# Summing one modulation vector off TensorE, and four others for one stream only

## The chip, the cores and the metric

The kernel runs on one core of a Trainium2 chip. The metric is the device time of one execution in microseconds (us). The kernel before took 1370.71 us, the median of three runs (1370.51 to 1374.48).

## What is computed

The reference is a block of two layers over two token streams of 256 tokens each: a latent stream `x` and a context stream `ctx`, 1024 channels wide. Layer 0 mixes tokens with a recurrence, layer 1 with a gated delta rule. Each is followed by a SwiGLU feed-forward part. Every sub-layer is modulated by vectors computed from `c` (latent) and `c_ctx` (context):

```python
for layer in range(DEPTH):                       # DEPTH = 2
    last = layer == DEPTH - 1
    mod_l = split((silu(c) @ ada_w[layer] + ada_b[layer])[:, None, :], 6)
    mod_c = split(silu(c_ctx) @ ada_w[layer] + ada_b[layer], 6)
    h_lat = modulate(rmsnorm(x, norm_g[layer, 0]), mod_l[0], mod_l[1])
    h_ctx = modulate(rmsnorm(ctx, norm_g[layer, 0]), mod_c[0], mod_c[1])
    ...                                          # the mixer gives y_lat, y_ctx
    x = x + mod_l[2] * y_lat
    x = x + mod_l[5] * swiglu(modulate(rmsnorm(x, norm_g[layer, 1]), mod_l[3], mod_l[4]), ...)
    if not last:
        ctx = ctx + mod_c[2] * y_ctx
        ctx = ctx + mod_c[5] * swiglu(...)
return rmsnorm(x, final_norm_g)
```

So each layer has six modulation vectors of 1024 channels for each of the two streams. Each is a product of an activation vector with a 1024 x 1024 slice of `ada_w`. In the last layer (layer 1) the context stream is read by the mixer but not carried on: vectors 0 and 1 of that layer are used for both streams, vectors 2 to 5 for the latent stream alone.

## The kernel before

Large products are made of three TensorE matmuls each (`mm3`): weights and activations are split into a high and a low part (`whi`/`wlo`, `hh`/`hl`), and high x high, high x low and low x high are summed. A weight tile of 128 x 1024 (512 KB) is loaded through SP's queue into one of three `raw` buffers, `whi` is a copy made on ScalarE or VectorE, `wlo` a subtraction made on VectorE or GpSimd (`weight`, line 704; two buffers of each). `product` (line 941) takes one such weight and runs 24 matmuls on it; with 512 tokens each is 128 x 512.

The program is recorded and then put in order in Python by a list scheduler (`Recorder`). It collects operations until a pool is closed (`flush`, line 391), chooses among the ready operations by an estimated time and their place in the program, and for operations with two possible engines (`scaled`: ScalarE or VectorE; `tt`: VectorE or GpSimd) also the engine. The order it gives on each engine, SP's DMA queue among them, is then fixed. All instructions are issued from one line, 612, so the profile's groups are told apart by the tiles they write and read.

Stages around the change: the first mixer (up to the close of pool `m0`, line 1095), whose end is the output projection, a norm and the first two weights of the feed-forward part; then the feed-forward part of layer 0, `ffn(0, ...)` (line 1098). It loops over 22 column tiles with a gate and an up product each (the first pair is made ahead, by `product2`), and then over eight output tiles of the down projection, each with weights of 8, 8 and 6 blocks, the last tile twice (once per half of the tokens). Its output is scaled by `mods[0][:, 5]` in `upd0`. Pool `fp` closes at line 1164; the second mixer follows.

The modulation vectors that are not needed at the very start are computed in the background. `ada_later(l, m...)` queues a generator `ada_steps(l, m)` per vector; each call of `product`, and each weight of a down projection, moves the first generator in the queue on by one step (`bg_step`). A vector has eight steps, one per 128 rows of its weight slice. A step loads 128 x 1024 of `ada_w` (512 KB) into a slot of `ring` (four slots in the first mixer, two in the feed-forward part) and then works in one of two ways:

- direct: four matmuls with the two activation columns (padded to 32) as the stationary operand, side by side in four column groups of TensorE, summed over the eight steps in one PSUM bank (`ps_ada<-ring,cs` in the profile);
- not direct: `acc` has one 128 x 1024 half for each stream (in the profile it goes by the name `x`, as it is part of the tile `x2`). The first step writes both halves by a scaling of the slot. Each later step does, for the latent stream, a multiply-add on VectorE; for the context stream, a scaling of the slot in place on ScalarE and an addition on VectorE or GpSimd. After the eighth step, eight matmuls with a selector as the stationary operand sum `acc` over the partitions (`ps_ada<-x,sel`).

The profile records each such 32-column matmul as two. Behind either way come a copy (`ada_ev`), two transposes (`ps_adat`) and an addition of the bias into `mods[l][:, m]`.

Before the change, vectors 2, 3, 4 and 5 of layer 0 are direct. (0,2) to (0,4) are queued with the mixer (line 1052). (0,5) is queued at line 1090; `bg_step(TUNE["g0"])`, with g0 = 4, records its first four steps in the first mixer's part, and the other four come in the feed-forward part. Layer 1's vectors 0 to 5 are queued at line 1131, not direct, and follow there.

Of the kernel before, what the change touches and what calls it, by code (L numbers as in the profile page):

```python
# [14 lines left out]
AF = mybir.ActivationFunctionType  # L15
OP = mybir.AluOpType
# [26 lines left out]
def _shuffle(sh, pattern, sizes):  # L43
# [18 lines left out]
    for g, n in zip(lhs, sh.shape, strict=True):  # L62
# [3 lines left out]
        for a in g:  # L66
# [7 lines left out]
TUNE = dict(warm=5000, ev=3000, stay=(300, 0), g0=4, early=(1, 2, 4, 6), eb=0, ea=(0, 1, 1, 1), nwo=2, prog=PROG,  # L74
            bias={'C3': -1500, 'N0': 100, 'N': -700, 'Z3': -1200, 'L': -1500, 'E3': 700, 'W': 10000, 'L3': -800, 'E': -300, 'W0': 10000, 'P': -100, 'E0': -300, 'N3': -700, 'P2': 0, 'C': 400, 'A': 700, 'Z': 700, 'C1': 0})
# [545 lines left out]
def hybrid_block(ctx: ExitStack, tc: tile.TileContext, I, out, dbg=None):  # L621
    nc = tc.nc
    ctx.enter_context(tc.manual_schedule())
    R = Recorder(tc, nc)
    T, V, S, G, sync = R.T, R.V, R.S, R.G, R.sync
# [14 lines left out]
    def bank(tag, name="ps"):  # L640
        if tag == "mm" and cur["wide"]:
            tag = ("mm", "tr", "st", "mm", "st", "tr", "st")[cur["turn"] % 7]
            cur["turn"] += 1
        return ps_pool.tile([128, 512], F32, tag=tag, bufs=banks[tag], name=name)

    def tmp(cols=512, dt=F32, name="tmp", tag="t2k", bufs=NB["t2k"]):
        t = tp.tile([128, 512], dt, tag=tag, bufs=bufs, name=name)
        return t[:, :cols] if cols != 512 else t
# [8 lines left out]
    def P(name):  # L657
        o, w = _SM[name]
        return sm[:, o:o + w]
# [23 lines left out]
    cs = cp.tile([128, NK, 32], F32, name="cs")  # L683
# [20 lines left out]
    def weight(*src, cols=1024, aside=False, place=None):  # L704

        r = raws.pop(0) if raws else raw_load(src, cols)
        hi, lo = place or (wp.tile([128, 1024], F32R, tag=t, bufs=NB[t], name=t) for t in ("whi", "wlo"))
        if aside:
            S.activation(hi[:, :cols], r[:, :cols], AF.Copy)
        else:  # L710
            R.copy(hi[:, :cols], r[:, :cols])
        (R.tt if (cur["wide"] or cur.get("flex")) and not aside else G.tensor_tensor)(lo[:, :cols], r[:, :cols], hi[:, :cols].bitcast(F32),
                                                                 OP.subtract)
        return hi, lo
# [3 lines left out]
    def ahead(*srcs):  # L718

        early.extend(weight(src, aside=True) for src in srcs)  # L720
# [13 lines left out]
    def ada_steps(l, m, direct=False):  # L734


        if l not in mods:
            mods[l] = cp.tile([128, 6, NK, 2], F32, name=f"mod{l}")
        if direct:
            ps = bank("ta", "ps_ada")  # L740
        for k in range(NK):
            r = next(cur["araw"])
            sync.dma_start(out=r, in_=I["ada_w"][l, m, k], after=cur["late"])
            if direct:
                for g in range(4):
                    T.matmul(ps[32 * g:32 * g + 32, 0:256], cs[:, k, :], r[:, 256 * g:256 * g + 256],
                             start=(k == 0), stop=(k == NK - 1))
            else:
                if k == 0:
                    acc = cur["acc"]  # L750
                    for v in range(2):
                        R.scaled(acc[:, v], r, cs[:, k, v:v + 1])
                else:
                    V.scalar_tensor_tensor(acc[:, 0], r, cs[:, k, 0:1], acc[:, 0], OP.mult, OP.add)
                    S.activation(r, r, AF.Copy, scale=cs[:, k, 1:2])
                    R.tt(acc[:, 1], acc[:, 1], r, OP.add)
            if k < NK - 1:
                yield
        if not direct:
            ps = bank("ta", "ps_ada")  # L760
            for v in range(2):
                for g in range(4):
                    T.matmul(ps[32 * g:32 * g + 32, 0:256], sel[:, v, :], acc[:, v, 256 * g:256 * g + 256],
                             start=(v == 0), stop=(v == 1))
        ev = tmp(256, name="ada_ev")
        S.activation(ev, ps[:, 0:256], AF.Copy)
        pt = bank("ta", "ps_adat")
        for t in range(2):
            T.transpose(pt[:, 128 * t:128 * t + 128], ev[:, 128 * t:128 * t + 128], ident)
        b = P("ada_b")[:, (l * 6 + m) * 8:(l * 6 + m) * 8 + 8]  # L770
        V.tensor_tensor(mods[l][:, m].rearrange("p (g t) v -> p g t v", t=2),
                        pt[:, 0:256].rearrange("p (t g c) -> p g t c", t=2, g=4)[:, :, :, 0:2],
                        b.rearrange("p (g t o) -> p g t o", t=2, o=1).to_broadcast([128, 4, 2, 2]), OP.add)
        yield

    def ada_later(l, *ms, direct=False):
        cur["bg"] += [ada_steps(l, m, direct) for m in ms]

    def bg_step(n=1):

        cur["quota"] -= n
        while n and cur["bg"] and cur["quota"] >= 0:
            if next(cur["bg"][0], "end") == "end":
                cur["bg"].pop(0)
            else:
                n -= 1
# [6 lines left out]
    def gain(l, which, m):  # L793
        a = cp.tile([128, NK, 2], F32, name=f"gain{l}{which}")
        o = (l * 2 + which) * 8
        V.scalar_tensor_tensor(a, mods[l][:, m], 1.0,
                               P("norm_g")[:, o:o + 8].rearrange("p (k o) -> p k o", o=1).to_broadcast([128, NK, 2]),
                               OP.add, OP.mult)
        return a
# [49 lines left out]
    def normed(xs, n, r, gn, shift, hh, hl):  # L849

        for i, c0 in enumerate(range(0, n, 256)):
            c = slice(c0, c0 + 256)
            for k in range(NK):
                ap, v = xs(k)[i]
                xg = tmp(256, name="xg")
                V.scalar_tensor_tensor(xg, ap, gn[:, k, v:v + 1], r[i], OP.mult, OP.mult)
                lift(k, c, xg, shift[:, k, v:v + 1], hh, hl)

    def both(t):
        return lambda k: [(t[:, k, 0:256], 1), (t[:, k, 256:512], 0)]  # L860
# [23 lines left out]
    for t in range(NK):  # L884
        ps = bank(("ta", "st")[t % 2], "ps_ada")
        for half in range(2):
            r = half_of[2 * t + half]
            sync.dma_start(out=r, in_=I["ada_w0"][t, half])
            for g in range(4):
                T.matmul(ps[32 * g:32 * g + 32, 0:256], cs[:, 4 * half + g, :], r[:, 256 * g:256 * g + 256],  # L890
                         start=half == 0, stop=half == 1)
# [195 lines left out]
        if len(parts) == 1:  # L1087
            r1.append(norm.part(cols.start))
    ahead(I["ffn_gu"][0, 0, 0], I["ffn_gu"][0, 1, 0])
    ada_later(0, 5, direct=True)  # L1090
    normed(both(x), 512, r1, gain(0, 1, 4), mods[0][:, 3], hh, hl)
    first = product2((I["ffn_gu"][0, 0, 0], I["ffn_gu"][0, 1, 0]), hh, hl)
    early.append(weight(I["ffn_gu"][0, 0, 1]))
    bg_step(TUNE["g0"])
    m0.close()


# [673 lines left out]
    r = norm.part(0)  # L1771
# [61 lines left out]
```

## Time and profile before

| | |
|---|---|
| three runs, median (lowest to highest) | 1370.71 us (1370.51 to 1374.48) |
| the profiled execution | 1377.74 us |
| its span, from the first to the last instruction | 1376.0 us |
| mean granted TensorE clock | 0.973 |
| busy share of the span: TensorE, VectorE, ScalarE, GpSimd | 96%, 77%, 43%, 18% |
| loads of `ada_w` | 96, of 512 KB |

How to read it: times are microseconds, engines are PE (TensorE matmuls), PEld (TensorE weight loads), DVE (VectorE), ACT (ScalarE), POOL (GpSimd) and SP (the queue that issues the DMAs). A row of the timeline has the start in us, the length in us, the engine, line, operation, written and read tiles, shape and count; in brackets stands the idle time of the engine before it and what ended that. A row of the table of stretches has the stretch, its length, the busy time and number of instructions of PE, PEld, DVE, ACT and POOL, the granted clock, the DMA share and GB/s. A row of one tile's instructions has the count, the shortest, median and longest duration in ns, and the first and last start in us. Matmuls overlap: the listed length of one is longer than the distance to the next.

### The profile page before, as it was taken

The page shows a single profiled execution, that of the slowest core. Times are in us where ns is not written, and L with a number is a line of the kernel's source. Part 1 is how long each engine was busy: PE and PEld are TensorE (multiplying, and loading weights), DVE is VectorE, ACT ScalarE, POOL GpSimd, SP SyncE. Part 2 cuts the span into 40 slices and gives each one's busy share as a digit, 9 for nine tenths or more (in the row PEclk, how much of TensorE's full clock was granted, in tenths as well). Part 3 has the DMA queues.
Part 4 walks back from the last instruction along what each step waited for, and adds up shares of the span by engine and source line. Part 5 has one row for each costly group of instructions (what it writes and reads, how often), then busy time and mean ns, then how long its engine had stood idle before and what let it go on. Part 6 is the DMA issues. An engine that isn't in the chain of part 4 may idle for free.

```text
span 1376.0 us, 23471 instructions
## 1 busy us (share of the span) xinstructions
PE 1324.9 (96%) x9280; PEld 1120.7 (81%) x9280; DVE 1055.5 (77%) x1856; ACT 591.5 (43%) x1078; POOL 247.3 (18%) x210
## 2 busy tenths in 40 slices
PE   6999999999999999999998999999998998999997
PEld 3677778778888888888867788898898888999997
DVE  5799986778887777457868889798599277777775
ACT  3388773334333333005745656747546341211100
POOL 2000000100121111212524333335243110000000
PEclk9999999999999999999999999999999599899999
DMA  9545443355555555233523222323133016355563
GB/s 356 193 166 179 139 152 121 122 179 191 203 179 184 186 192 172 84 111 124 173 75 124 74 78 79 107 82 107 61 119 117 20 55 206 131 184 184 180 181 115
DMA packets 61262, 195.62 MB, mean 142 GB/s; under 512 B 6752, under 2 KB 9952, under 8 KB 60896
## 3 DMA queue, kind: packets, MB, share of 16 engines
q1 hardware_dynamic: 61152, 194.12, 42.5%
q8 instruction: 73, 1.20, 0.4%
q14 instruction: 37, 0.30, 0.1%
HBM read 184.13 MB, written 9.96 MB: 141 GB/s over the span
## 4 chain that ended last, share of the span: by engine, by line
PE 56%; issue 16%; DVE 6%; ACT 3%; DMA 1%; POOL 0%; POOLq 0%; SPq 0%; ACTq 0%; DVEq 0%
PE ps_mm L612 28%; PE ps_dn L612 9%; PE ps_e L612 2%; PE ps_y L612 2%; PE ps_wo L612 2%; PE ps_z L612 2%; PE ps_w L612 2%; PE ps_s L612 2%; PE ps_ks L612 1%; DVE lw L612 1%; PE ps_a L612 1%; PE ps_qs L612 1%; DVE cu L612 1%; PE ps_o L612 1%; DMA ring<-ada_w 1%
## 5 line engine op out<-in xcount | busy, mean ns | idle before, releaser
L612 PE MATMUL ps_mm<-hh,whi 128*128 128x512 f32 (+1 forms) x888 | 328.3, 372 | 7.1 <-DVE cu L612 5.6
L612 PE MATMUL ps_mm<-hh,wlo 128*128 128x512 f32 (+1 forms) x888 | 327.8, 370 | 4.0 <-DVE wlo L612 2.3
L612 PE MATMUL ps_mm<-hl,whi 128*128 128x512 f32 (+1 forms) x888 | 327.1, 370 | 0.5 <-DVE hl L612 0.3
L612 DVE TENSOR_TENSOR wlo<-raw,whi 128x1024 fp32r<-128x1024 f32 (+2 forms) x185 | 233.8, 1264 | 21.6 <-ACT whi L612 13.3
L612 DVE CAST whi<-raw 128x1024 fp32r<-128x1024 f32 (+1 forms) x172 | 116.9, 679 | 129.2 <-PE ps_mm L612 68.7
L612 PEld LDWEIGHTS ps_mm<-hh,whi 128*128 128x128 f32 x888 | 170.3, 193 | 41.2 <-issue 9.6
L612 PEld LDWEIGHTS ps_mm<-hh,wlo 128*128 128x128 f32 x888 | 170.9, 193 | 33.8 <-DVE wlo L612 3.6
L612 PEld LDWEIGHTS ps_mm<-hl,whi 128*128 128x128 f32 x888 | 170.7, 193 | 26.5 <-issue 1.6
L612 POOL TENSOR_TENSOR wlo<-raw,whi 128x1024 fp32r<-128x1024 f32 x53 | 127.1, 2399 | 356.3 <-DVE whi L612 193.4
L612 PE MATMUL ps_dn<-fh,whi 128*128 128x256 f32 (+1 forms) x374 | 122.6, 328 | 0.0
L612 PE MATMUL ps_dn<-fl,whi 128*128 128x256 f32 (+1 forms) x374 | 122.6, 328 | 0.0
L612 PE MATMUL ps_dn<-fh,wlo 128*128 128x256 f32 (+1 forms) x374 | 122.3, 327 | 0.0
L612 PE MATMUL ps_mm<-h2h,whi 128*128 128x256 f32 x352 | 101.1, 288 | 1.1 <-ACT h2h L612 1.1
L612 PE MATMUL ps_mm<-h2l,whi 128*128 128x256 f32 x352 | 101.2, 287 | 0.0
L612 PE MATMUL ps_mm<-h2h,wlo 128*128 128x256 f32 x352 | 100.6, 286 | 0.0
L612 ACT ACTIVATE whi<-raw 128x1024 fp32r<-128x1024 f32 (+2 forms) x66 | 68.1, 1031 | 63.7 <-PE ps_mm L612 33.2
L612 ACT ACTIVATE fh<-sg 128x256 fp32r<-128x256 f32 (+1 forms) x43 | 22.5, 523 | 145.2 <-DVE sg L612 145.1
L612 ACT ACT_TABLE_LOAD x59 | 75.7, 1283 | 7.0 <-DMA sm<-small 3.4
L612 PEld LDWEIGHTS ps_dn<-fh,whi 128*128 128x128 f32 x374 | 71.1, 190 | 6.8 <-issue 0.4
L612 PEld LDWEIGHTS ps_dn<-fh,wlo 128*128 128x128 f32 x374 | 71.1, 190 | 6.1
L612 PEld LDWEIGHTS ps_dn<-fl,whi 128*128 128x128 f32 x374 | 71.1, 190 | 6.0
L612 ACT ACTIVATE ring<-ring,cs 128x1024 f32<-128x1024 f32 x42 | 48.3, 1150 | 64.4 <-DVE x L612 64.4
(326 smaller groups left out, 2637.9 us busy)
## 6 DMA issues: line engine op xcount, KB each, us to landing
ring<-ada_w SPq DMA_DIRECT2D x96, 512.0 KB, 4.5
raw<-ffn_gu SPq DMA_DIRECT2D x88, 512.0 KB, 3.6
raw<-dn_w_in SPq DMA_DIRECT2D x49, 512.0 KB, 3.5
raw<-ffn_down SPq DMA_DIRECT2D x34, 512.0 KB, 3.5
raw<-rg_w_in SPq DMA_DIRECT2D x16, 512.0 KB, 4.5
raw<-ffn_down SPq DMA_DIRECT2D x17, 384.0 KB, 3.4
raw<-dn_w_out SPq DMA_DIRECT2D x12, 512.0 KB, 3.9
raw<-rg_w_out SPq DMA_DIRECT2D x10, 512.0 KB, 3.5
```

The source lines that it names most:

```text
L612: call(*[real(x) for x in args], **{n: real(v) for n, v in kw.items()})
```

## The change

Vector (0,5) is no longer direct, and all its eight steps come in the feed-forward part, ahead of those of layer 1. For vectors 2 to 5 of layer 1, only the latent half of `acc` is computed and summed; the context columns of these vectors then hold the bias alone and are not read.

```diff
@@ ada_steps
+        nv = 1 if l == 1 and m >= 2 else 2
...
                 if k == 0:
                     acc = cur["acc"]
-                    for v in range(2):
+                    for v in range(nv):
                         R.scaled(acc[:, v], r, cs[:, k, v:v + 1])
                 else:
                     V.scalar_tensor_tensor(acc[:, 0], r, cs[:, k, 0:1], acc[:, 0], OP.mult, OP.add)
-                    S.activation(r, r, AF.Copy, scale=cs[:, k, 1:2])
-                    R.tt(acc[:, 1], acc[:, 1], r, OP.add)
+                    if nv == 2:
+                        S.activation(r, r, AF.Copy, scale=cs[:, k, 1:2])
+                        R.tt(acc[:, 1], acc[:, 1], r, OP.add)
...
-            for v in range(2):
+            for v in range(nv):
                 for g in range(4):
                     T.matmul(ps[32 * g:32 * g + 32, 0:256], sel[:, v, :], acc[:, v, 256 * g:256 * g + 256],
-                             start=(v == 0), stop=(v == 1))
+                             start=(v == 0), stop=(v == nv - 1))
@@ ahead of the feed-forward part
-    ada_later(0, 5, direct=True)
+    ada_later(0, 5)
     normed(both(x), 512, r1, gain(0, 1, 4), mods[0][:, 3], hh, hl)
     first = product2((I["ffn_gu"][0, 0, 0], I["ffn_gu"][0, 1, 0]), hh, hl)
     early.append(weight(I["ffn_gu"][0, 0, 1]))
-    bg_step(TUNE["g0"])
     m0.close()
```

## The prediction

> **What bounds the kernel now.** I read the page's busy line and slices first, then the busy time by stretch for the stages that the edit touches.
>
> ```profile
> PE 1324.9 (96%) x9280; PEld 1120.7 (81%) x9280; DVE 1055.5 (77%) x1856; ACT 591.5 (43%) x1078; POOL 247.3 (18%) x210
> ...
> 225.00:245.00 20.00, 20.00 (x149) 18.37 (x148) 15.65 (x23) 8.41 (x15) 3.87 (x3) 1.00 0.37 119
> 245.00:262.00 17.00, 14.55 (x97) 14.11 (x97) 15.26 (x38) 8.46 (x19) 3.07 (x3) 0.80 0.28 109
> 262.00:307.00 45.00, 42.98 (x208) 32.47 (x206) 28.84 (x33) 12.01 (x15) 2.41 (x1) 1.00 0.50 167
> 307.00:503.00 196.00, 196.00 (x911) 159.38 (x912) 158.14 (x152) 74.57 (x87) 30.50 (x12) 1.00 0.57 190
> 503.00:552.00 49.00, 49.00 (x241) 39.16 (x240) 36.93 (x41) 15.98 (x21) 6.60 (x3) 1.00 0.56 174
> ```
>
> TensorE (second column: busy PE) is full from 307 to 552 us, to the hundredth; from 262 to 307 it lacks 2.0 us. VectorE is at 81% there (158.14 of 196), ScalarE at 38%, the DMA at 57%. So in this stage, the first feed-forward part (about 262 to 630), only what leaves TensorE's own stream shortens the run. What matters for one matmul is its start-to-start distance, not its listed length:
>
> ```profile
> 325.61 0.39 PE L612 MATMUL ps_mm<-hh,whi 128*128 128x512 f32 x1
> 325.84 0.39 PE L612 MATMUL ps_mm<-hl,whi 128*128 128x512 f32 x1
> 326.07 0.39 PE L612 MATMUL ps_mm<-hh,wlo 128*128 128x512 f32 x1
> 326.29 0.39 PE L612 MATMUL ps_mm<-hh,whi 128*128 128x512 f32 x1
> ```
>
> Three steps take 0.68, one 0.227 us, though each is listed at 0.39. A product of 24 takes 5.44 us. Anything put between two of these costs the distance it adds.
>
> **The change part by part.**
>
> *The direct steps of vector (0,5) go.* There are eight, each with four calls, recorded as eight half-passes. Two of the three places:
>
> ```profile
> 194.23 0.39 PE L612 MATMUL ps_mm<-ol,whi 128*128 128x512 f32 x1
> 194.55 1.48 PE L612 MATMUL ps_ada<-ring,cs 128*32 128x256 f32 x18
> 195.96 0.50 PE L612 MATMUL ps_mm<-oh,wlo 128*128 128x512 f32 x1
> 196.30 0.40 PE L612 MATMUL ps_mm<-oh,whi 128*128 128x512 f32 x1
> ...
> 200.28 0.39 PE L612 MATMUL ps_mm<-ol,whi 128*128 128x512 f32 x1
> 200.60 0.63 PE L612 MATMUL ps_ada<-ring,cs 128*32 128x256 f32 x6
> 201.16 0.51 PE L612 MATMUL ps_mm<-oh,wlo 128*128 128x512 f32 x1
> 201.50 0.40 PE L612 MATMUL ps_mm<-oh,whi 128*128 128x512 f32 x1
> ...
> 268.63 0.39 PE L612 MATMUL ps_mm<-hl,whi 128*128 128x512 f32 x1
> 268.94 0.64 PE L612 MATMUL ps_ada<-ring,cs 128*32 128x256 f32 x8
> 269.51 0.50 PE L612 MATMUL ps_mm<-hh,wlo 128*128 128x512 f32 x1
> 269.85 0.39 PE L612 MATMUL ps_mm<-hh,whi 128*128 128x512 f32 x1
> ```
>
> From the matmul before a batch to the second one after it should be two distances, 0.454. At 194 it is 2.07, so 18 half-passes cost 1.62; at 200 it is 1.22, so six cost 0.77: three steps for 2.39 us. The four steps of the feed-forward part cost 0.77 each (269.85 - 268.63 - 0.454), 3.07 in all. The fourth step falls here:
>
> ```profile
> 243.23 0.64 PE L612 MATMUL ps_ada<-ring,cs 128*32 128x256 f32 x8
> ...
> 247.42 1.02 PE L612 MATMUL ps_ms<-ncol,sq 128*128 128x1 f32 x4 [2.32 <-ACT sq L612]
> ```
>
> TensorE idles 2.32 us behind it for the norm, so it fills a gap; I take nothing (at most 0.77). Removed: 2.39 + 3.07 = 5.46 us.
>
> *One summing batch for (0,5) comes, and four of layer 1 are halved.* A batch with both streams has 16 half-passes:
>
> ```profile
> 373.35 0.39 PE L612 MATMUL ps_mm<-hh,whi 128*128 128x512 f32 x1
> 373.66 1.07 PE L612 MATMUL ps_ada<-x,sel 128*32 128x256 f32 x16
> 374.67 0.50 PE L612 MATMUL ps_mm<-hl,whi 128*128 128x512 f32 x1
> 375.01 0.40 PE L612 MATMUL ps_mm<-hh,wlo 128*128 128x512 f32 x1
> ```
>
> 1.66 less 0.454 is 1.21 us, added once. One with the latent stream alone has eight half-passes of the same shape as a direct step, 0.77, so each of the four saves 0.44: 1.76 us. The copy, two transposes and addition behind a batch stay, one set per vector.
>
> [...]
>
> **Sum: -5.46 + 1.21 - 1.76 = -6.0 us.**
>
> *What VectorE, ScalarE and GpSimd get instead.* A two-stream step is one multiply-add on VectorE, one scaling on ScalarE, one addition on VectorE or GpSimd:
>
> ```profile
> L612 DVE SCALAR_TENSOR_TENSOR x<-ring,cs,x x42: 1272/1280/3282, 290.4 to 539.8; 128x1024 f32<-128x1024 f32 x42
> L612 ACT ACTIVATE ring<-ring,cs x42: 1135/1152/1158, 291.7 to 541.1; 128x1024 f32<-128x1024 f32 x42
> L612 DVE TENSOR_TENSOR x<-x,ring x29: 1210/1217/2543, 294.5 to 542.3; 128x1024 f32<-128x1024 f32 x29
> L612 POOL TENSOR_TENSOR x<-x,ring x13: 2396/2407/3157, 302.7 to 497.5; 128x1024 f32<-128x1024 f32 x13
> ```
>
> (0,5) adds seven multiply-adds, scalings and additions and two first products; layer 1 loses 28 scalings, 28 additions and four first products. Multiply-adds go from 42 to 49, scalings and additions from 42 to 21. The steps all move eight products earlier, to start near 266 rather than 280.4. In 262 to 307 four or five more steps of 1.28 + 1.22 add about 11 us to VectorE's 28.84 of 45: 40, or 88%, still under TensorE. I cost them at nothing because TensorE's products cover them, as they covered 42 such steps from 290 to 542 at one visible loss:
>
> ```profile
> 302.75 2.41 POOL L612 TENSOR_TENSOR x<-x,ring 128x1024 f32<-128x1024 f32 x1 [50.12 <-ACT ring L612]
> 303.38 2.32 DVE L612 TENSOR_TENSOR fl<-sg,fh 128x512 fp32r<-128x512 f32 x1 [0.70 <-ACT fh L612]
> ...
> 306.89 0.50 PE L612 MATMUL ps_mm<-hh,wlo 128*128 128x512 f32 x1 [1.12 <-DVE wlo L612]
> ```
>
> An addition on GpSimd stretched VectorE's subtraction for `fl` to 2.32 us, the next `wlo` came late, and TensorE lost 1.12. That is the price if the cover fails; -1.12 if this stall goes with its new place.
>
> *The moved transfers.* Four of vector (0,5)'s eight 512 KB loads leave SP's queue ahead of 190 us and go behind 243 us, among the `ffn_gu` weight loads; the count stays. A load waits in SP's queue for its ring slot, with weights queued behind it; in the light steps the slot is free after the multiply-add alone. From 262 to 307 the DMA is at 50%, and waits for the ring ended beside full products:
>
> ```profile
> 290.39 1.28 DVE L612 SCALAR_TENSOR_TENSOR x<-ring,cs,x 128x1024 f32<-128x1024 f32 x1 [5.31 <-DMA ring<-ada_w]
> ```
>
> VectorE waited 5.31 us here and TensorE did not stop. Cover is one product, 5.44 us. I take nothing; the bounds are a stall as above, 1.12, per late weight, and the 1.12 at 306.89 won back.
>
> *The new wait.* TensorE now waits for the last addition into the accumulator instead of ring loads; products queue behind it. The batches of layer 1 already have this wait, inside the measured 1.21, so nothing more.
>
> **From the profile to the median.** The profiled execution took 1377.74 us (span 1376.0), 7.0 above the median 1370.71. The sum is matmul time, the same in both: 1371.7 against the profiled one, **1364.7** against the median.
>
> **Rivals.**
>
> *Clock gate: 1368.1 or 1361.3.* After TensorE's waits for norms the granted clock drops: 0.80 over 245 to 262 above, a loss of 0.20 x 17 = 3.4 us, and here:
>
> ```profile
> 1170.00:1180.00 10.00, 8.88 (x44) 7.92 (x43) 8.55 (x21) 4.53 (x10) 0.00 (x0) 0.59 0.04 15
> ```
>
> 0.41 x 10 = 4.1 us. These are waits after which one more or one less slow spell of the size of the first, 3.4, is possible once work ahead of them is 2.4 or 6 us shorter. For: the two losses differ after similar waits. Against: the waits are unchanged. [...]
>
> *The front share stays: 1367.1.* The 2.39 us saved at 194 to 201 lie ahead of the norm at 238 to 248, which ends on VectorE, ScalarE and GpSimd. If that chain, not TensorE, sets 247.42, only -3.6 is left. Against: TensorE is busy 20.00 of 20 from 225 to 245, and VectorE waits between its groups there.
>
> *Nothing comes out: 1370.7.* The change fails to do its work if the batches already lie in waits. The rows around them show no such wait except at 243.
>
> *Slower: VectorE becomes the bound at the start of the feed-forward part.* If additions there block VectorE as at 302.75, each `wlo` comes 1.12 late. 21 additions remain; nine such stalls (10.1 us) take back 6.0 and make it slower by over 0.3%, or 4.1 us; all 21 cost 23.5 and give 1388. For: the steps start closer to the first products, when whi and wlo are just caught up. Against: of 42 additions before, 13 on GpSimd, one stalled TensorE by 1.12.
>
> **How the numbers follow.** The measurement tells about 0.3%, 4.1 us, from no change: faster is below 1366.6, slower above 1374.8. Forecast 0.56 (1362.5 to 1366.9; 0.50 faster, 0.06 same); clock 0.18 (0.08 down, faster; 0.10 up, same); front share stays 0.16 (0.04 faster, 0.12 same); nothing 0.04 (same); slower 0.06. Faster 0.62, same 0.32, slower 0.06. The range, 1360.5 to 1369.0, spans the forecast with one such stall more or less, the retained front share and both clock cases; it leaves out nothing-comes-out and slower, 0.10, and edges.
>
> **What would show it.** `ps_ada<-ring,cs` falls from 384 records to 320, `ps_ada<-x,sel` from 96 to 80 (three batches of 16, four of 8), scalings from 42 to 21. A batch of eight costs 0.77. The first matmul of the down projection comes 5.1 earlier than 502.9 (the sum without the two halved batches that fall behind it):
>
> ```profile
> L612 PE MATMUL ps_dn<-fh,whi x374: 276/283/504, 502.9 to 1364.8; 128*128 128x256 f32 x110, 128*128 128x512 f32 x77
> ```
>
> What makes it wrong: PE waits for `wlo` between 262 and 400 beyond 2 us in all, a granted clock that differs from 0.80 and 0.59 at the two places, or a new order of the norm ahead of 248.

## The result and the profile after

| | before | after |
|---|---|---|
| median of 13 runs each | 1374.32 us (1369.78 to 1382.15) | 1363.96 us (1355.40 to 1368.69) |
| ratio, 95% interval | | 0.9932 (0.9912 to 0.9952) |
| the profiled execution, its span | 1377.74, 1376.0 us | 1364.68, 1363.0 us |

The ratio is a gain of 9.3 us, between 6.6 and 12.1. The forecast was 6.0 us off 1370.71, the median of the first three runs; over 13 runs the kernel before came to 1374.32. That the changed kernel's 1363.96 lies 0.7 us from the forecast time of 1364.7 is therefore partly luck: the starting point was 3.6 too low and the gain 3.3 larger than forecast, and the forecast gain of 6.0 lies just outside the measured interval.

The busy line of the page, the summing batches by tile, and the busy time by stretch, all of the changed kernel:

```profile
PE 1308.6 (96%) x9200; PEld 1110.3 (81%) x9200; DVE 1035.0 (76%) x1851; ACT 564.9 (41%) x1053; POOL 229.6 (17%) x203
...
L612 PE MATMUL ps_ada<-ring,cs x320: 379/403/637, 14.0 to 187.9; 128*32 128x256 f32 x160
L612 PE MATMUL ps_ada<-x,sel x80: 379/379/403, 301.3 to 565.5; 128*32 128x256 f32 x80
```
```profile
243.00:260.00 17.00, 13.86 (x85) 12.87 (x85) 16.01 (x39) 8.46 (x19) 3.84 (x3) 0.80 0.33 123
260.00:302.00 42.00, 42.00 (x201) 34.60 (x200) 35.20 (x35) 17.65 (x20) 4.80 (x2) 1.00 0.54 180
302.00:497.50 195.50, 195.50 (x901) 158.40 (x902) 138.60 (x148) 51.01 (x67) 10.00 (x4) 1.00 0.59 194
497.50:567.00 69.50, 69.50 (x319) 56.40 (x318) 41.58 (x48) 8.76 (x15) 9.60 (x4) 1.00 0.54 170
```

The 384 and 96 records became 320 and 80. TensorE is still full from 260 us on, while VectorE went from 81% to 71% (138.60 of 195.50) and ScalarE from 38% to 26%: most of what the other engines gained has no use there, and the time came from TensorE's stream, a few short waits for those engines included (below).

To see where the 13.0 us between the two spans lie, I cut both traces at the small instruction `rs` on GpSimd, which ends each norm. First the kernel before, then after:

```profile
248.71 0.70 POOL L612 TENSOR_TENSOR rs<-ms,nhalf 128x2 f32<-128x2 f32 x1 [2.08 <-DVE ms L612]
...
631.97 0.89 POOL L612 TENSOR_TENSOR rs<-ms,nhalf 128x2 f32<-128x2 f32 x1
```
```profile
247.09 0.71 POOL L612 TENSOR_TENSOR rs<-ms,nhalf 128x2 f32<-128x2 f32 x1 [1.67 <-DVE ms L612]
...
625.88 0.91 POOL L612 TENSOR_TENSOR rs<-ms,nhalf 128x2 f32<-128x2 f32 x1
```

Three stretches are compared from here on: the *front* (from the first `ps_mm<-oh` matmul, at 194.0 and 193.8, to the first of these `rs`), the *feed-forward part* (between the two) and the *rest* (from the second to the end of the span). The kernel before and the changed kernel were each traced three times, once with 40 idle-time matmuls added to the changed one (below):

| trace | front | feed-forward part | rest |
|---|---|---|---|
| before | 54.7, 54.7, 54.7 | 383.3, 382.3, 383.5 | 744.0, 741.6, 744.1 |
| after | 53.3, 53.4, 53.2 | 378.8, 378.2, 378.8 | 737.1, 739.5, 737.6 |
| difference of the means | -1.4 | -4.4 | -5.2 |

Front and feed-forward part repeat to 0.2 and 1.2 us and give -5.8. In the rest every engine has the same instructions in both kernels, and but for TensorE's matmuls of its first 13 us in the same order, so next to nothing that the change does is seen there; yet it differs.

### The profile page after: what moved, and what is told of

Read it like the earlier page. It is cut to its first block, busy times and chain, and to the rows that moved or that the text cites. A ratio compares the mean times of both kernels' runs of the same rounds, so it can differ in the third digit from the quotient of the medians.

```text
span 1363.0 us, 23260 instructions
## 1 busy us (share of the span) xinstructions
PE 1308.6 (96%) x9200; PEld 1110.3 (81%) x9200; DVE 1035.0 (76%) x1851; ACT 564.9 (41%) x1053; POOL 229.6 (17%) x203
## 3 DMA queue, kind: packets, MB, share of 16 engines
q8 instruction: 72, 1.18, 0.4%
## 4 chain that ended last, share of the span: by engine, by line
PE 56%; issue 15%; DVE 6%; ACT 4%; DMA 1%; POOL 0%; POOLq 0%; SPq 0%; ACTq 0%; DVEq 0%
PE ps_mm L612 29%; PE ps_dn L612 9%; PE ps_e L612 2%; PE ps_wo L612 2%; PE ps_y L612 2%; PE ps_w L612 2%; PE ps_z L612 2%; PE ps_s L612 1%; DVE lw L612 1%; PE ps_ks L612 1%; DVE cu L612 1%; PE ps_a L612 1%; PE ps_qs L612 1%; PE ps_o L612 1%; ACT gn L612 1%
## 5 line engine op out<-in xcount | busy, mean ns | idle before, releaser
L612 DVE TENSOR_TENSOR wlo<-raw,whi 128x1024 fp32r<-128x1024 f32 (+2 forms) x183 | 220.5, 1205 | 17.4 <-ACT whi L612 8.3
L612 DVE CAST whi<-raw 128x1024 fp32r<-128x1024 f32 (+2 forms) x177 | 120.2, 679 | 145.8 <-PE ps_mm L612 81.0
L612 POOL TENSOR_TENSOR wlo<-raw,whi 128x1024 fp32r<-128x1024 f32 x55 | 132.0, 2402 | 506.5 <-DVE whi L612 351.3
L612 ACT ACTIVATE whi<-raw 128x1024 fp32r<-128x1024 f32 (+2 forms) x61 | 63.2, 1036 | 77.8 <-PE ps_mm L612 45.1
L612 DVE SCALAR_TENSOR_TENSOR x<-ring,cs,x 128x1024 f32<-128x1024 f32 x49 | 63.9, 1304 | 15.4 <-DMA ring<-ada_w 14.4
```

The source lines that it names most:

```text
L612: call(*[real(x) for x in args], **{n: real(v) for n, v in kw.items()})
```

## Experiments

Ratios are against the kernel before, run beside each on the same chip.

### Controls

The kernel before, unchanged (twice), and the changed kernel, unchanged.

> The kernel before once more, unchanged, as a control. Three stretches are read from its trace: the front (first ps_mm<-oh matmul to the second rs of the norm, 54.7 us in the profile of before, 53.3 after), the feed-forward part (from there to the rs at 632: 383.3 before, 378.8 after) and the rest (to the end: 744.0 before, 737.1 after). In the rest every engine has the same instructions in the same order in both kernels. Theory A: the 6.9 us of the rest are chance (how the clock gate's spells and one 2.4 us hole fall in one execution); then this trace's rest differs from 744 by several us, most likely shorter, and its front and feed-forward part stay within 0.5 of 54.7 and 383.3. Theory B: they belong to the kernel (the place of its instructions in memory); then the rest is 744 within 1.5 us and the 2.44 us hole ahead of ps_z is there again. Timed: same within the interval, ratio 1.000.

> The changed kernel once more. Both theories: front 53.3 and feed-forward part 378.8 within 0.5. Theory A: the rest differs from 737.1 by several us, most likely longer, about 740. Theory B: 737.1 within 1.5. Timed: about 0.993 to 0.996; by the sum of the prediction 0.9956, by all 13 runs so far 0.993.

> The kernel before a third time, for the surplus in the rest. If it belongs to the kernel: 79.6 us again from the nkh at 959 to the fo at 1038 (slow clock spell), rest 741 to 744. If it was chance: 78.4 there and a rest of 737 to 740. Timed: 1.000.

Measured: 0.9989 (0.9967 to 1.0011) and 0.9982 (0.9955 to 1.0008) for the kernel before; 0.9924 (0.9895 to 0.9953) for the changed one. Front and feed-forward part came out as expected, but for 1.0 and 0.6 us in the latter. The controls' intervals reach from a gain of 6.2 us to a loss of 1.5 where nothing differs, so a timed difference of two thousandths means nothing here; the stretches of the traces tell much smaller differences apart. The rest of the kernel before stayed the longer one with repetition: 741.6 and 744.1, against 739.5. By the expectations the 741.6, without the 2.44 us hole, and the 739.5 speak for theory A, the 744.1 for theory B. What the rest goes with is shown below, under "The rest".

### One half of the change at a time

```diff
-        nv = 1 if l == 1 and m >= 2 else 2       # in the changed kernel
+        nv = 2
```

> Only the first half of the change: vector (0,5) off TensorE, layer 1 for both streams in all six vectors. My steps: front as after, 53.3 (-1.4); feed-forward part 383.3 - 3.07 + 1.21 = 381.4, and 380.3 if the 1.12 us stall at 306.89 goes because the steps lie elsewhere. Rival (VectorE at its limit with 55 two-stream steps in a row): stalls for wlo of 1.1 us each appear and the feed-forward part stays at 383 or above. Timed by the sum: 1374 - 1.4 - 1.9 to -3.0, ratio about 0.997.

Measured: 0.9945 (0.9924 to 0.9966); front 53.5, feed-forward part 381.5 (expected 381.4). No series of stalls came with 56 two-stream steps in a row: one wait of 0.95 us for `wlo`, at 558.83. The 381.5 is met in part by luck: beside that wait, two of this kernel's batches were split in two (0.33 us more each), and waits that the kernel before has early in this part are gone (they stand under "Why the prediction was right").

```diff
-    ada_later(0, 5)                              # in the changed kernel
+    ada_later(0, 5, direct=True)
...
+    bg_step(TUNE["g0"])
     m0.close()
```

> Only the second half: vectors 2 to 5 of layer 1 for the latent stream alone, (0,5) direct as before. My steps: front 54.7 unchanged; feed-forward part 383.3 - 1.76 = 381.5, the stall at 306.89 still there, as vectors 0 and 1 lie where they did. [...] If the relief of VectorE, ScalarE and GpSimd were worth anything by itself, it would be below 381. Timed: ratio about 0.9987.

Measured: 0.9958 (0.9932 to 0.9984); front 54.7, feed-forward part 381.9 (expected 381.5), with the stall still there, at 307.21 and 1.42 long. Against the mean of before, 383.0, the halves give 1.5 and 1.1, together 2.6, and the whole 4.4: each half keeps a stall for `wlo` (0.95 and 1.42) that the whole is rid of.

### The front: direct, but in the feed-forward part

```diff
-    bg_step(TUNE["g0"])                          # in the kernel before
     m0.close()
```

> The kernel before with vector (0,5) still direct, but all eight steps in the feed-forward part (the call that records four of them in the mixer is left out). It separates the front from the rest of the change. If the three steps ahead of the norm cost the 2.39 us of the prediction and all of it comes out, the front falls from 54.7 to 52.3. If, as the traces of the changed kernel say, their batch partly covered a wait of TensorE for wlo, 53.3 again, with that wait of about 0.7 at 195 us there. Feed-forward part, by either: 382.8 + 4 x 0.77 = 385.9. Sum 439.2 to 438.2, against 437.5 before.

Measured: 0.9990 (0.9967 to 1.0013); front 53.5, feed-forward part 385.6 (expected 385.9). One row of this trace's TensorE timeline decides between the two fronts, and the changed kernel has its like:

```profile
192.16 0.50 PE L612 MATMUL ps_mm<-oh,wlo 128*128 128x512 f32 x1 [0.74 <-DVE wlo L612]
```
```profile
194.05 0.39 PE L612 MATMUL ps_mm<-ol,whi 128*128 128x512 f32 x1
195.16 0.51 PE L612 MATMUL ps_mm<-oh,wlo 128*128 128x512 f32 x1 [0.72 <-DVE wlo L612]
195.51 0.40 PE L612 MATMUL ps_mm<-oh,whi 128*128 128x512 f32 x1
```

Before, the batch of 18 stood between these matmuls and cost 1.62. Without it TensorE waits for `wlo`, which VectorE makes between the scans of the mixer: 195.51 - 194.05 - 0.454 = 1.0 of the 1.62 stays.

### The stall at 306.89: all additions on VectorE, or all on GpSimd

```diff
-                    R.tt(acc[:, 1], acc[:, 1], r, OP.add)             # in the kernel before
+                    V.tensor_tensor(acc[:, 1], acc[:, 1], r, OP.add)
```

> The kernel before with all 42 additions into the accumulator on VectorE (13 were on GpSimd). The stall of 1.12 us at 306.89 was put down to an addition on GpSimd that holds VectorE's subtraction. If so, it is gone: front 54.7, feed-forward part 381.2 to 382.3. Rival (VectorE is simply full there): the stall stays or grows, as VectorE has 13 x 1.22 us more: 383 to 386. This kernel has the instructions of before on TensorE in the same order and number, so it also tests the slow clock spell around 960 to 970 us that both traces of before have and no other: if it belongs to the count on TensorE, it is here (79.6 us from the nkh at 959 to the fo at 1038), otherwise 78.4.

Measured: 0.9979 (0.9953 to 1.0005); front 54.7, feed-forward part 381.7, and no stall at that place. That alone would not settle the cause, as the stall is missing from some traces without this edit too. Of the three traces of before two have it (1.12 and 1.18); the third, whose addition held `fl` for 1.53 instead of 2.32 us, has none, and is 1.1 shorter in that part. Three more traces have the same order here: where `fl` took 2.31 and 2.32 us TensorE stalled for 1.42 (vectors 2 to 5 for one stream) and 0.57 (48 matmuls ahead, below), and where it took 1.51 (16 ahead) it did not. Here `fl` takes 0.68. So the stall goes with a held `fl` in all seven. The slow clock spell near 960 is not there (78.45), though TensorE's instructions are those of before.

```diff
-                        R.tt(acc[:, 1], acc[:, 1], r, OP.add)         # in the changed kernel
+                        G.tensor_tensor(acc[:, 1], acc[:, 1], r, OP.add)
```

> The changed kernel with all 21 additions into the accumulator on GpSimd (4 are there now). The slower rival: each holds VectorE's two-operand work for up to 2.4 us, wlo comes late, TensorE stalls 1.1 us for many of them: feed-forward part 378.5 + up to 17 x 1.1 = 397, ratio up to 1.006. My steps: 17 times 1.2 us leave VectorE and the plan fits other work beside them, so a few stalls at most: 378.5 to 381, ratio 0.993 to 0.995.

Measured: 0.9968 (0.9945 to 0.9991); front 53.7, feed-forward part 382.05, 3.5 more than the changed kernel and above my 381. Three waits of TensorE account for 2.8 of it (the third is 0.25, at 390.54). Two of them, and what VectorE met ahead of the second (the timelines of TensorE, and of GpSimd and VectorE):

```profile
303.44 0.64 PE L612 MATMUL ps_ada<-x,sel 128*32 128x256 f32 x8 [1.89 <-DVE x L612]
322.76 0.50 PE L612 MATMUL ps_mm<-hh,wlo 128*128 128x512 f32 x1 [0.65 <-DVE wlo L612]
```
```profile
316.10 5.52 POOL L612 TENSOR_TENSOR x<-x,ring 128x1024 f32<-128x1024 f32 x2 [8.99 <-ACT ring L612]
316.48 2.89 DVE L612 CAST whi<-raw 128x1024 fp32r<-128x1024 f32 x1
319.48 3.23 DVE L612 TENSOR_TENSOR wlo<-raw,whi 128x1024 fp32r<-128x1024 f32 x1
```

Two additions in a row held the copy for `whi` (0.69 elsewhere) and the subtraction for `wlo` (1.2 elsewhere): the copy, begun 0.38 after the first addition, took 2.89, and the subtraction took 3.23 and ended at 322.71, 1.09 after the second. How an addition holds them no run shows. The wait of 1.89 is the one that the prediction calls the new wait: TensorE's summing batch stands in its queue until the accumulator is written. So the slower rival's mechanism is real, at 3.5 us for 17 more additions on GpSimd, 0.2 each, not 1.1.

### The rest: instructions ahead that do nothing

```diff
+    pad = bank("ta", "ps_pad")
+    for i in range(16):                          # 48; 40 in the changed kernel
+        T.matmul(pad[0:32, 0:32], ones[0:32, 0:32], ones[0:32, 32:64], start=True, stop=True)
     cs = cp.tile([128, NK, 32], F32, name="cs")
```

> The kernel before with 16 tiny matmuls (32x32 on ones, about 0.06 us each) at the very start, where TensorE waits for its first data; nothing else moves on any engine. So far all three variants (the change and its halves) came out about 4.5 us better than their front and feed-forward part explain, and the surplus lies in the rest, where all instructions are the same. Theory B (the place of the instructions in memory, that is how many stand ahead on TensorE's queue): a different count ahead moves the time of this kernel too: ratio 0.996 to 0.998 with front 54.7 and feed-forward part 382 to 383 unchanged. Theory A (chance in the comparison): 1.000, rest 740 to 744.

> The same with 48 tiny matmuls, about 2.7 us of TensorE in its wait at the start. Theory B: another place of the instructions, so again a ratio off 1.000 by some 0.3%, either way. Theory A: 1.000. Both: front 54.7, feed-forward part 382 to 383.

> The changed kernel with 40 tiny matmuls at the start: as many matmul records again as in the kernel before (9280), so the second mixer's instructions on TensorE stand where they stood before. Theory B, by TensorE's queue alone: the surplus goes, the rest is 741 to 744 and the ratio about 0.996. Theory A, or a cause that is not TensorE's count: rest 737 to 740, ratio 0.992 to 0.994 as without the pad. Both: front 53.3, feed-forward part 378.5.

Measured: 0.9973 (0.9950 to 0.9995), 0.9981 (0.9956 to 1.0006) and 0.9937 (0.9917 to 0.9958). Front and feed-forward part did not move (437.0, 438.0 and 432.0 in sum). The rest is 738.4, 738.1 and 737.6. So the two padded traces of the kernel before lie 3 to 6 us below the three without a pad, and the changed kernel does not become longer when TensorE's record count is put back to 9280: the count on that queue is not the cause. The pads were longer than the expectations say: each tiny matmul is two records about 0.06 us apart, so 16 take 1.9 us and 48 take 5.3.

What the rest goes with is the granted clock, which falls to 0.50 in spells of 3.4 us or a multiple (in the first trace of before 3.41 us from 632.09, 6.82 from 959.77 and 34.13 from 1062.17, among others). From 10 us windows of before and of before_pad16, at the same `nkh` of the second mixer:

```profile
958.97:968.97 10.00, 9.71 (x240) 9.09 (x241) 6.34 (x15) 8.16 (x18) 4.88 (x5) 0.66 0.26 83
```
```profile
954.12:964.12 10.00, 8.60 (x257) 7.78 (x257) 7.63 (x19) 9.35 (x21) 4.90 (x5) 1.00 0.23 83
```

The granted clock is 0.66 against 1.00 (third number from the end). All three traces of before have such a spell at this place (0.66, 0.66, 0.83; 0.6 to 1.2 us longer from there to the `fo` at 1038), and none of the eleven others. More of the difference lies between 1038 and 1123, where the clock is low around rows of tiny matmuls in every trace (78 to 85 us). First before, then after, between the same two `fo`:

```profile
1038.61:1122.83 84.22, 77.55 (x828) 71.57 (x827) 49.67 (x114) 40.46 (x82) 17.88 (x20) 0.80 0.17 55
```
```profile
1029.79:1108.53 78.74, 73.74 (x828) 68.01 (x827) 49.78 (x114) 40.40 (x82) 17.94 (x21) 0.85 0.17 59
```

The next stretch shows it within one kernel. It is the kernel before in its first and second trace, from a copy for `whi` to a subtraction for `wlo`:

```profile
1132.22:1163.40 31.18, 28.92 (x237) 28.31 (x236) 23.67 (x34) 2.87 (x7) 0.73 (x1) 1.00 0.61 206
```
```profile
1122.98:1157.45 34.47, 31.51 (x237) 30.90 (x236) 23.67 (x33) 2.87 (x7) 0.73 (x1) 0.90 0.55 189
```

Over all fourteen traces this stretch takes 29.8 to 31.6 us with no slow spell in it, 32.4 to 32.9 with one of 3.4 us and 34.3 to 35.3 with 6.8. Where no trace has a spell they agree better: within 0.3 us in three stretches of 29, 64 and 160 us, and within 1.6 in one of 212. Summed over the rest:

| traces | rest | of it at half clock |
|---|---|---|
| before | 744.0, 741.6, 744.1 | 68, 54, 58 us |
| after | 737.1, 739.5, 737.6 | 47, 50, 51 us |
| before with 16 and 48 matmuls ahead | 738.4, 738.1 | 50, 44 us |
| the six others | 733.7 to 741.3 | 36 to 50 us |

On average the kernel before spends 10.5 us more at half clock, by estimate a loss of 5.2 us, and its rest is 5.2 us longer. So close a match is luck: a single trace's rest less that estimate runs from 710.0 to 716.6. These 5.2 us are not work that the change saves. A half clock makes the same matmuls longer (28.92 and 31.51 us of busy TensorE in the two rows above), but what starts the spells, and why the kernel before gets more of them, stays open. Neither the pad nor the change is needed to be rid of the one near 960 (all additions on VectorE was enough). The timed runs cannot settle it: the padded kernels' 0.9973 and 0.9981 are not told from the controls' 0.9989 and 0.9982.

### A step further: sums in pairs

Vectors 2 and 3, and 4 and 5, of layer 1 use the two halves of `acc`, and one batch, copy and pair of transposes serves both.

```diff
+        lone = l == 1 and m >= 2                 # in the changed kernel
+        h = m % 2 if lone else 0
...
-                    V.scalar_tensor_tensor(acc[:, 0], r, cs[:, k, 0:1], acc[:, 0], OP.mult, OP.add)
+                    V.scalar_tensor_tensor(acc[:, h], r, cs[:, k, 0:1], acc[:, h], OP.mult, OP.add)
...
+        if lone and not h:
+            yield
+            return
...
+        if lone:                                 # writes mods[l][:, m - 1:m + 1, :, 0]
```

> The changed kernel, carried on: vectors 2 and 3, and 4 and 5, of layer 1 are summed as pairs, each in one half of the accumulator; one batch of 16 half-passes, one copy and two transposes for a pair instead of two batches of eight with four transposes. My steps: 4 x 0.77 becomes 2 x 1.21 (-0.66), and two pairs of transposes go (about 0.23 each, -0.46): feed-forward part 378.5 - 1.1 = 377.4. Rival: hidden, 378.5. Timed: 0.992 to 0.993, not to be told from the changed kernel.

Measured: median 1359.40 us, 0.9888 (0.9857 to 0.9918); front 53.2, feed-forward part 377.7, 0.9 less than the changed kernel where 1.1 was expected. The second pair's batch was split into two of eight, so the batches gave 0.33 of the 0.66; with two pairs of transposes at 0.22 each that is 0.8 of the 0.9. Its rest, 733.7, is the shortest of all traces, and that it beats the changed kernel by more than the 0.9 is not shown: the changed kernel's own ratios run from 0.9924 to 0.9937. Against the kernel before its interval leaves no doubt.

## Why the prediction was right

**The place.** TensorE's own stream bounds the stage, and all else is covered: held in the main. Short waits for the other engines went as well, about 1.1 us of them (under "Nothing for VectorE"). The sum of the two stretches that the change touches is -5.8 against the forecast -6.0. The first down-projection matmul came at 497.7, 5.2 earlier; 5.1 was forecast.

**A batch of eight at 0.77.** Held. In the changed kernel, for vector (1,2):

```profile
435.56 0.39 PE L612 MATMUL ps_mm<-hh,wlo 128*128 128x512 f32 x1
435.88 0.64 PE L612 MATMUL ps_ada<-x,sel 128*32 128x256 f32 x8
436.45 0.50 PE L612 MATMUL ps_mm<-hh,whi 128*128 128x512 f32 x1
436.79 0.39 PE L612 MATMUL ps_mm<-hl,whi 128*128 128x512 f32 x1
```

1.23 less 0.454 is 0.78. Halving a batch gained: 0.78 stands against the 1.21 of sixteen half-passes. The four direct steps in the feed-forward part were priced right too: with all eight there each still costs 0.77 or 0.78, and the part is 2.6 longer (385.6 against 383.0), where 3.07 was expected.

**One batch for (0,5) at 1.21.** Mis-sized: the planner split it into two batches of eight, one per stream as each accumulator half became ready (the first at 301.25 us, the second at 304.32), so 2 x 0.77 = 1.54.

**The front at 2.39.** Mis-sized: 1.4 came out, as the batch at 194 stood partly in a wait for `wlo`. I had read the matmuls on both sides as back to back, which they were, because of the batch. The forecast had this as a rival, for another reason (the norm) and as all or nothing; the norm passed on what it was given.

**Nothing for VectorE.** Held and more. With -3.07, +1.54 and -1.76 the feed-forward part would be -3.3; it is -4.4. The remaining 1.1 are TensorE's waits, which the prediction put at nothing with bounds of 1.12 either way. The stall at 306.89 (in two of three traces of before, 0.77 on average) is gone in all three of the changed kernel. So are two short waits at the first products, of 0.9 together, in all three traces of before; two new ones, of 0.82 together, stand just behind the norm in two of the three after. First before, then after:

```profile
262.63 0.50 PE L612 MATMUL ps_mm<-hh,whi 128*128 128x512 f32 x1 [0.31 <-DVE whi L612]
263.96 0.50 PE L612 MATMUL ps_mm<-hh,wlo 128*128 128x512 f32 x1 [0.59 <-DVE wlo L612]
```
```profile
247.78 0.58 PE L612 MATMUL ps_mm<-hl,whi 128*128 128x256 f32 x1 [0.48 <-DVE hl L612]
250.41 1.19 PE L612 MATMUL ps_rs<-dg,ones 128*128 128x256 f32 x2 [0.34 <-DVE dg L612]
```

With the averages over three traces each, -3.29 - 0.77 - 0.90 + 0.55 is -4.41. The two misses of the forecast, 1.0 less in front and 0.8 more behind, cancel. That the sum is closer than its terms is luck.

**Slower rival.** Shown to exist, and small: forcing it cost 3.5 us.

**Clock rival.** It came true in the traces beside the forecast, not in its place: the rest is 5.2 us shorter, with 10.5 us less at half clock, where one slow spell more or less (3.4) was allowed. That a spell sits at one place in all traces of one kernel, and in no other, I had not allowed for. Of the three signs of being wrong, no wait for `wlo` falls between 262 and 400, and the norm's work ahead of 248 kept its order on VectorE and GpSimd. The clock is 0.80 at the first place again but 0.75 at the second, in the 10 us from 1157.21, where it was 0.59; in the three traces of before alone it runs from 0.59 to 0.70 there, so this sign says nothing.

The timed gain, 9.3 us, lies above the -5.8 of the traced stretches; its interval begins at 6.6. Of the surplus of 3.5, 1.5 to 2.5 us may be the comparison itself, as copies of the kernel before measure 0.9989 and 0.9982; the clock may hold the others. In the two comparisons for which all clocks are on record, the changed kernel ran at a mean granted clock of 0.979 and 0.980, the kernel before beside it at 0.977 and 0.978.

## What to carry to other kernels

On a full TensorE, price small batches by the start-to-start distance of the large matmuls around them, and do not expect half of a batch to cost half: here eight half-passes cost 0.77 us and sixteen 1.21. Before counting a batch as saved, ask what TensorE would wait for at that place without it: the engine that makes its next weight may be just behind (here a wait for `wlo` kept 1.0 of 1.62 us). Cut the traces of two kernels at a marker that both have, and repeat the unchanged kernel: here the stretch that the change could not touch differed as much as the one that it did. Read the granted clock of such a stretch before giving its time to the change.

## What the runs showed of the hardware

A one-operand copy on VectorE was held by GpSimd's additions just as the two-operand subtraction was: 2.89 us instead of 0.69, beside 3.23 instead of 1.2, with all additions on GpSimd. And slow spells of the clock can recur with a program: one of 3.4 or 6.8 us (0.66 to 0.83 over 10 us) stood at the same place in all three traces of the kernel before and in none of the eleven others, where the work from there on is the same. Two of those had only tiny matmuls added in a wait at the start, some 950 us ahead, and one had only 13 additions moved from GpSimd to VectorE, 460 us ahead or more. What starts or ends such a spell was not found.
